# Seven products in place of eight for part of the w_up and gate multiplications of a two-layer encoder trunk

## The chip, the cores and the metric

The kernel runs on one NeuronCore of a Trainium2 chip. The metric is the device time of one execution in microseconds (us); lower is better. TensorE (PE in the profile) multiplies, VectorE (DVE) and ScalarE (ACT) work element by element, GpSimd (POOL) is all but unused here, and the queue of SyncE (SP) issues the loads of the weights.

## What is computed

Two layers of an encoder over 256 tokens of width 2048, all in float32. Cut to what matters here:

```python
proj = x @ w_in                       # 2048 x 10240; its last 4096 columns are gate_A and gate_B
...                                   # two attentions A and B on the other columns
mix = (sigmoid(gate_A) * (A @ w_pa) + sigmoid(gate_B) * (B @ w_pb)) @ w_out
x = layer_norm(alpha * x + mix)
gate, up = split(x @ w_up)            # 2048 x 11264: 5632 columns each
x = layer_norm(alpha * x + (silu(gate) * up) @ w_down)
```

## The kernel before

**Float32 from three products.** Each float32 operand is split into a high part, which TensorE's fast float32 format (fp32r) holds, and a low part, the difference. A product is high x high, high x low and low x high: three matmuls, with x (transposed, 128 features by 128 tokens) as the stationary operand and 512 columns of a weight as the moving one (`rows_product`, lines 215 to 217).

**Pieces.** All the weights are cut into 960 pieces of 512 KB (128 x 1024 a piece), one list in program order. `run` walks it: for piece m it first emits the split of the piece AHEAD_SPLIT places on (`split_to`: ScalarE copies the high part, line 128, VectorE subtracts for the low part, line 129), then the matmuls of piece m, then `post`, what reads a finished accumulator, and then one step of `background`, a list of small tasks (attention, transposes of finished blocks by `turn_block`, the affine step of a LayerNorm). Loads run up to AHEAD_LOAD pieces further on, in a ring of N_RAW buffers. Each engine takes its instructions strictly in this emitted order.

**Buffers.** Split parts, x, transposed blocks and more share N_UNITS units of 4 KB a partition; a writer waits for the last reader of what lay in its unit. PSUM has eight banks: two accumulators of two banks each (one bank for each half of the tokens), which alternate from one multiplication to the next, and four single banks (`aux`) for transposes and attention.

**The places that change.** In `w_up`, chunk c of 512 columns takes the gate block (8 pieces, then silu) and the up block (8 pieces, then the product, line 752); the result is transposed (`turn_block`, line 402; copy and low part at lines 290 and 291, called hT) as the input of `w_down`. `w_down` runs in two parts, after chunks 5 and 10; `residual_gemm` adds to the residual `res`. Where a LayerNorm follows, the last 256 columns are done first for tokens 0 to 127 and then for tokens 128 to 255 (`gemm_a_halves`), so that the first half's LayerNorm lies beside the second half's matmuls. The gates take two such multiplications of 8 pieces for each of four chunks, followed by `merge`: 2 pieces of w_pa and 4 of w_pb. An affine step of two VectorE instructions for each of eight pieces of `res` (lines 436 and 437) is left over for the background in the chunks of `w_up`.

Of the kernel before, what the change touches and what calls it, by code (L numbers as in the profile page):

```python
# [43 lines left out]
EARLY = 3  # L44


def bias_tables():
# [29 lines left out]
def trunk(ctx: ExitStack, tc: tile.TileContext, x, rel_bias, w_in, sink, w_pa, w_pb, w_out,  # L77
# [26 lines left out]

    pieces = []
    background = []
    state = {"load": 0, "split": 0}
    norms = []

    def piece(src, kk, cc, mm, pre=None, post=None):  # L110
        pieces.append(dict(src=src, kk=kk, cc=cc, mm=mm, pre=pre, post=post))
        return pieces[-1]

    def load_to(m):
        while state["load"] < min(m, len(pieces)):
            pc = pieces[state["load"]]
            pc["raw"] = work.tile([P, pc["kk"], pc["cc"]], F32, name="raw", tag="raw", bufs=N_RAW)
            nc.sync.dma_start(pc["raw"], pc["src"])
            state["load"] += 1

    def split_to(m):
        while state["split"] < min(m, len(pieces)):
            load_to(state["split"] + 1 + AHEAD_LOAD)
            pc = pieces[state["split"]]
            raw = pc["raw"]
            hi = unit([P, pc["kk"], pc["cc"]], F32R, "whi")
            lo = unit([P, pc["kk"], pc["cc"]], F32R, "wlo")
            nc.scalar.activation(hi, raw, AF.Copy)  # L128
            nc.vector.tensor_tensor(out=lo, in0=raw, in1=hi.bitcast(F32), op=ALU.subtract)  # L129
            pc["hi"], pc["lo"] = hi, lo  # L130
            state["split"] += 1

    def flush():
        while background:
            background.pop(0)()

    def run():

        for m, pc in enumerate(pieces):
            ahead = min(AHEAD_SPLIT, 1 + m)  # L140
            for n in norms:
                if n - 24 <= m < n:
                    ahead = max(ahead, min(n - m + AHEAD_NORM, AHEAD_SPLIT + (m - n + 24) // 3))
            split_to(m + 1 + ahead)
# [105 lines left out]
    def gemm_a_halves(w, k0, k1, c0, width, xs, post, between):  # L250

        kk = 1024 // width
        st = {"w": []}

        def part(t, j, pc):
            if j == k0:
                st["acc"] = acc_tile()
            for k in range(kk):
                rows_product(st["acc"], t, width, xs(j + k), pc["hi"][:, k, :], pc["lo"][:, k, :],
                             j + k == k0, j + k == k1 - 1)  # L260

        def mm(j, pc):
            part(0, j, pc)
            st["w"].append((j, pc))
            if j + kk >= k1:
                post(0, st["acc"])
                for a in st["w"][:-1]:
                    part(1, *a)
                between()
                part(1, *st["w"][-1])  # L270
                post(1, st["acc"])
        for j in range(k0, k1, kk):
            src = w[j * P:(j + kk) * P, c0:c0 + width].rearrange("(k p) c -> p k c", p=P)
# [133 lines left out]
    def ln_scale(stats, t):  # L407
# [241 lines left out]
    def layer(l, xt, pre, turn, after_last):  # L649
# [67 lines left out]
        def gate(c):  # L717
            for nm, c0 in (("a", GA), ("b", GB)):
                def post(acc, nm=nm):
                    sg[nm] = work.tile([P, 2, 512], F32, name="sg", tag="sg", bufs=3)  # L720
                    nc.scalar.activation(sg[nm], acc, AF.Sigmoid)
                gemm_a(wi, 0, KT, c0 + 512 * c, 512, xs, post)

        def merge(c):
            def post_a(acc):
                nc.vector.tensor_tensor(out=sg["a"], in0=sg["a"], in1=acc, op=ALU.mult)

            def post_b(acc):
                nc.vector.tensor_tensor(out=sg["b"], in0=sg["b"], in1=acc, op=ALU.mult)
                nc.vector.tensor_tensor(out=sg["a"], in0=sg["a"], in1=sg["b"], op=ALU.add)  # L730
                turn_block(sg["a"], mt, "mT")
            gemm_a(w_pa[l], 0, 4, 512 * c, 512, lambda kt: lookup(oa)(kt), post_a, pre=([flush] if c == 0 else None))
            gemm_a(w_pb[l], 0, 8, 512 * c, 512, lambda kt: lookup(ob)(kt), post_b)

        for c in range(4):
            gate(c)
            merge(c)
# [16 lines left out]

        stats2 = small.tile([P, 2, 5, 6], F32, name="stats", tag="stats", bufs=2)
        after2, between2, ret = after_last(stats2)
        for half, (c0, c1) in enumerate(((0, 6), (6, 11))):
            for c in range(c0, c1):
                st = {}
                gemm_a(w_up[l], 0, KT, 512 * c, 512, x1s, lambda acc, st=st: post_gate(acc, st),  # L760
                       turn=(turn1 if c == 0 else None))
                gemm_a(w_up[l], 0, KT, D_FF + 512 * c, 512, x1s, lambda acc, st=st: post_up(acc, st))
            residual_gemm(w_down[l], 4 * c0, 4 * c1, lookup(hs), ALPHA if half == 0 else None,
                          None if half == 0 else stats2, after2, between2)
        if l < DEPTH - 1:
            norms.append(len(pieces))
        return ret
# [80 lines left out]
```

## Time and profile before

| | |
|---|---|
| median of three runs | 2767.43 us (2766.91 to 2768.36) |
| profiled execution | 2767.28 us, span 2765.5 us |
| PE busy | 2749.0 us (99%), 13539 matmuls |
| DVE busy | 1480.9 us (54%) |
| ACT busy | 1168.2 us (42%) |
| granted TensorE clock | 0.998 |

A busy PE is not yet a PE at its peak, since its matmuls overlap: one lasts 390 ns in the profile, while the next starts 227 ns after it. What a matmul costs is therefore read from the starts, not from the durations. Rows with "x6" merge six instructions that follow each other, and the time beside them reaches from the start of the first to the end of the last.

### The profile page before, as it was taken

To read this page: it belongs to the slowest core of one execution; us is meant where nothing else is said; L and a number is where in the kernel's file an instruction comes from. 1 tells how busy PE (TensorE), PEld (TensorE's weight loads), DVE (VectorE), ACT (ScalarE), POOL (GpSimd) and SP (SyncE) were. 2 spreads that over 40 slices of the span, in tenths; PEclk is the share of its full clock that TensorE was granted. 3 is DMA by queue.
4 is the path that set the end of the run, shared out by engine and by line. 5 is a ranking of instruction groups with operands and counts; after the bars stand their busy time and mean duration, and the time that the engine had idled before them with its cause. 6 is when DMAs were issued, how large, how long until landed. Compare 5 with 4: busy or idle time off the path is not lost.

```text
span 2765.5 us, 34763 instructions
## 1 busy us (share of the span) xinstructions
PE 2749.0 (99%) x13539; PEld 2319.5 (84%) x13539; DVE 1480.9 (54%) x1688; ACT 1168.2 (42%) x1407; POOL 5.4 (0%) x13
## 2 busy tenths in 40 slices
PE   9999999999999999999999999999999999999998
PEld 7888888888888888888889888888888888888887
DVE  5566554566644544445566655455665444444445
ACT  4454443444333443434344544433544344423441
POOL 0000000000000000000000000000000000000000
PEclk9999999999999999999999999999999999999999
DMA  8866665564655554655656666555645565555554
GB/s 255 241 183 181 185 202 178 187 229 149 225 184 183 208 204 158 211 177 191 215 162 201 179 183 191 177 201 179 232 162 198 183 205 205 183 183 183 187 209 145
DMA packets 359801, 531.84 MB, mean 192 GB/s; under 512 B 52288, under 2 KB 153664, under 8 KB 359636
## 3 DMA queue, kind: packets, MB, share of 16 engines
q1 hardware_dynamic: 358836, 528.31, 58.1%
q8 instruction: 106, 1.74, 0.3%
q10 hardware_dynamic: 800, 1.31, 0.1%
q14 instruction: 59, 0.48, 0.0%
HBM read 522.86 MB, written 6.68 MB: 191 GB/s over the span
## 4 chain that ended last, share of the span: by engine, by line
PE 98%; DVE 1%; DMA 0%; SPq 0%; issue 0%; ACT 0%; DVEq 0%; POOL 0%; ACTq 0%; POOLq 0%
PE acc L217 27%; PE acc L215 27%; PE acc L216 27%; PE acc L202 9%; PE acc L171 5%; PE aux L402 1%; PE aux L297 0%; PE aux L296 0%; PE aux L295 0%; DVE xT L392 0%; PE aux L562 0%; PE aux L528 0%; PE aux L620 0%; PE aux L544 0%; DMA res<-in_x_dram 0%; PE aux L370 0%
## 5 line engine op out<-in xcount | busy, mean ns | idle before, releaser
L129 DVE TENSOR_TENSOR wlo<-raw,whi 128x1024 fp32r<-128x1024 f32 x960 | 1127.4, 1221 | 474.5 <-ACT whi L128 455.4
L128 ACT ACTIVATE whi<-raw 128x1024 fp32r<-128x1024 f32 x960 | 971.5, 1054 | 434.9 <-DMA raw<-in_w_down_dram 142.1
L215 PE MATMUL acc<-whi,xT 128*128 128x512 f32 (+1 forms) x2176 | 848.7, 390 | 0.0
L217 PE MATMUL acc<-whi,xT 128*128 128x512 f32 (+1 forms) x2176 | 842.0, 387 | 0.0
L216 PE MATMUL acc<-wlo,xT 128*128 128x512 f32 (+1 forms) x2176 | 840.8, 386 | 0.0
L217 PEld LDWEIGHTS acc<-whi,xT 128*128 128x128 f32 x2176 | 409.1, 188 | 84.2
L215 PEld LDWEIGHTS acc<-whi,xT 128*128 128x128 f32 x2176 | 409.3, 188 | 80.8 <-issue 0.7
L216 PEld LDWEIGHTS acc<-wlo,xT 128*128 128x128 f32 x2176 | 409.4, 188 | 80.5
L202 PE MATMUL acc<-xT,whi 128*128 128x512 f32 x1088 | 387.0, 399 | 0.0
L171 PE MATMUL acc<-xT,wlo 128*128 128x256 f32 x1088 | 299.6, 280 | 0.0
L215 PE MATMUL acc<-whi,hT 128*128 128x512 f32 (+1 forms) x784 | 288.9, 368 | 0.0
L217 PE MATMUL acc<-whi,hT 128*128 128x512 f32 (+1 forms) x784 | 288.2, 368 | 0.0
L216 PE MATMUL acc<-wlo,hT 128*128 128x512 f32 (+1 forms) x784 | 288.0, 367 | 0.0
L202 PEld LDWEIGHTS acc<-xT,whi 128*128 128x128 f32 x1088 | 203.0, 188 | 43.3
L171 PEld LDWEIGHTS acc<-xT,wlo 128*128 128x128 f32 x1088 | 205.6, 189 | 2.6
L215 PEld LDWEIGHTS acc<-whi,hT 128*128 128x128 f32 x784 | 147.8, 189 | 24.3
L216 PEld LDWEIGHTS acc<-wlo,hT 128*128 128x128 f32 x784 | 147.9, 189 | 24.3
L217 PEld LDWEIGHTS acc<-whi,hT 128*128 128x128 f32 x784 | 147.8, 189 | 24.3
L290 ACT ACTIVATE hT<-aux 128x512 fp32r<-128x512 f32 x44 | 26.3, 598 | 315.2 <-PE aux L402 315.2
L752 DVE TENSOR_TENSOR sg<-sg,acc 128x1024 f32<-128x1024 f32 x22 | 26.9, 1221 | 202.3 <-PE acc L217 202.3
L215 PE MATMUL acc<-whi,mT 128*128 128x512 f32 (+1 forms) x320 | 111.5, 348 | 0.0
L217 PE MATMUL acc<-whi,mT 128*128 128x512 f32 (+1 forms) x320 | 111.0, 347 | 0.0
(133 smaller groups left out, 1503.8 us busy)
## 6 DMA issues: line engine op xcount, KB each, us to landing
raw<-in_w_up_dram SPq DMA_DIRECT2D x352, 512.0 KB, 4.7
raw<-in_w_in_dram SPq DMA_DIRECT2D x320, 512.0 KB, 4.9
raw<-in_w_down_dram SPq DMA_DIRECT2D x176, 512.0 KB, 5.5
raw<-in_w_out_dram SPq DMA_DIRECT2D x64, 512.0 KB, 5.6
raw<-in_w_pb_dram SPq DMA_DIRECT2D x32, 512.0 KB, 5.0
raw<-in_w_pa_dram SPq DMA_DIRECT2D x16, 512.0 KB, 5.9
bias<-ftab SPq DMA_DIRECT2D x96, 64.0 KB, 3.7
ftab<-fb SPq DMA_DIRECT2D x7, 640.0 KB
```

Source lines behind the costliest of these rows:

```text
L128: nc.scalar.activation(hi, raw, AF.Copy)
L129: nc.vector.tensor_tensor(out=lo, in0=raw, in1=hi.bitcast(F32), op=ALU.subtract)
L171: nc.tensor.matmul(st["acc"][:, n, 0:SEQ], lhsT=lo[:, k, n * P:(n + 1) * P], rhs=xs(4 * j + k)[:, 0, :], start=False, stop=False)
L202: nc.tensor.matmul(acc, lhsT=hi[:, k, n * P:(n + 1) * P], rhs=xs(kt).rearrange("p h t -> p (h t)"), start=first and not turn, stop=last)
L215: nc.tensor.matmul(o, lhsT=xk[:, 0, ts], rhs=hi, start=first, stop=False)
L216: nc.tensor.matmul(o, lhsT=xk[:, 0, ts], rhs=lo, start=False, stop=False)
L217: nc.tensor.matmul(o, lhsT=xk[:, 1, ts], rhs=hi, start=False, stop=last)
L290: nc.scalar.activation(hi, src, AF.Copy)
L402: nc.tensor.transpose(out=ps[:, k, t * P:(t + 1) * P], in_=src[:, t, c0:c0 + P], identity=ident)
L752: nc.vector.tensor_tensor(out=s, in0=s, in1=acc, op=ALU.mult)
```

## The change

The gate block and the up block of one chunk (and gate_A and gate_B of one) are computed together by a new function, `gemm_s`. It takes the 16 row tiles of the weight in eight pairs. With two row tiles, two halves of the tokens and two column blocks, a pair is a product of two 2 x 2 matrices of blocks: eight block products, 24 matmuls. Three of the eight pairs ("S" in PLAN) are done by Strassen's method (Winograd's form) with seven products, 21 matmuls; the five others ("C") as before. An S pair is four entries in the list of pieces, two with a load and two without. VectorE makes the sums of the weight's blocks (t13, t24) and their low parts; the sums of x (`sum_rows`) are made once for each x. The seven products go to all eight banks: q1, q5, q6, q7 to the four aux banks, q2 and q3 to one accumulator, q4 and x (the fourth plain result) to the other. After the last S pair, `fold` turns q1, q5, q6 and q7 into four corrections (e, f), and after the last pair each of the four banks is added to its correction (line 414). In the S pairs and the C pairs between them no background step runs ("quiet").

26 of the 30 pairs of blocks are done in this way: chunks 1 to 10 of `w_up` and chunks 1 to 3 of the gates, in both layers. Besides, the splits run five pieces ahead in place of three, with seven raw buffers and 36 units; transposes of finished blocks go into a list of their own that is served first (`soon`); and `w_down` runs in three parts (4, 4 and 3 chunks) in place of two, so the last part, with its 256-column ends, has 12 row tiles in place of 20.

```diff
-N_RAW = 6
-N_UNITS = 37
+N_RAW = 7
+N_UNITS = 36
+SUMS = 3
+PLAN = "SCSCSCCC"
-AHEAD_SPLIT = 3
+AHEAD_SPLIT = 5
...
-            if background:
-                background.pop(0)()
+            if not pc.get("quiet") and (soon or background):
+                (soon or background).pop(0)()
...
+        names = {"S": ("q1", "q2", "q3", "q5", "q7", "q6", "q4"),
+                 "C": ("q2", "q2", "q4", "q4", "q3", "q3", "x", "x")}
...
+            def split1(pc):
+                split_plain(pc)
+                b["left"] = pc["raw"]
+            def split2(pc):
+                raw = b["right"] = pc["raw"]
+                b["t13"] = unit([P, 2, 512], F32, "t13")
+                nc.vector.tensor_tensor(out=b["t13"][:, 0, :], in0=b["left"][:, 0, :], in1=raw[:, 0, :], op=ALU.add)
+                b["b22"] = unit([P, 2, 512], F32R, "b22")
+                split_into(b["b22"][:, 0, :], b["b22"][:, 1, :], raw[:, 1, :])
...
+            def split3(pc):
+                b["t24"] = unit([P, 2, 512], F32, "t24")
+                for o, x0, x1 in ((b["t13"][:, 1, :], b["right"][:, 0, :], b["right"][:, 1, :]),
+                                  (b["t24"][:, 0, :], b["t13"][:, 0, :], b["right"][:, 1, :])):
+                    nc.vector.tensor_tensor(out=o, in0=x0, in1=x1, op=ALU.add)
+                nc.vector.tensor_tensor(out=b["t24"][:, 1, :], in0=b["t24"][:, 0, :], in1=b["left"][:, 1, :], op=ALU.add)
+                b["h13"] = halves(b["t13"])
+            def split4(pc):
+                b["h24"] = halves(b["t24"])
...
+        def fold():
+            e, f, d = unit([P, 2, 512], F32, "e"), unit([P, 2, 512], F32, "f"), work.tile([P, 512], F32, name="tmp", tag="tmp", bufs=2)
+            nc.scalar.activation(e[:, 0, :], st["q1"], AF.Copy)
+            nc.vector.tensor_tensor(out=d, in0=e[:, 0, :], in1=st["q6"], op=ALU.subtract)
+            nc.vector.tensor_tensor(out=e[:, 1, :], in0=d, in1=st["q7"], op=ALU.subtract)
+            nc.vector.scalar_tensor_tensor(f[:, 0, :], st["q5"], -1.0, d, op0=ALU.mult, op1=ALU.subtract)
+            nc.vector.scalar_tensor_tensor(f[:, 1, :], st["q5"], -1.0, e[:, 1, :], op0=ALU.mult, op1=ALU.subtract)
...
+                for t, n in enumerate(names_):
+                    for k in range(2):
+                        product(n, rows(2 * p + k, t), pc["hi"][:, k, :], pc["lo"][:, k, :])
+                    if last:
+                        nc.vector.tensor_tensor(out=out_[:, t, :], in0=st[n], in1=st[extra][:, t, :], op=ALU.add)
...
-        background.extend([lambda: None, lambda: half(0), lambda: half(1)])
+        soon.extend([lambda: None, lambda: half(0), lambda: half(1)])
...
-        for half, (c0, c1) in enumerate(((0, 6), (6, 11))):
+        chunks = ((0, 4), (4, 8), (8, 11))
+        for part, (c0, c1) in enumerate(chunks):
             for c in range(c0, c1):
                 st = {}
...
+                if c > 0:
+                    gemm_s(w_up[l], 512 * c, D_FF + 512 * c, x1s, sums, post_both)
+                    continue
```

**TensorE at the end of a chunk of w_up.** Before, the next block starts in the other accumulator at once (acc_7032 is the finished one).

```order
L215 MATMUL acc_7032<-whi_7101,xT_5502 128x512
L216 MATMUL acc_7032<-wlo_7102,xT_5502 128x512
L217 MATMUL acc_7032<-whi_7101,xT_5502 128x512
L215 MATMUL acc_7178<-whi_7119,xT_5495 128x512
L216 MATMUL acc_7178<-wlo_7120,xT_5495 128x512
L217 MATMUL acc_7178<-whi_7119,xT_5495 128x512
```

Now (acc_8145 and acc_8146 are the banks of this chunk, acc_8501 and acc_8502 the same two pairs of banks for the next one, b22, thi and tlo the high and low parts of the weight's sums, sT a sum of x):

```order
L331 MATMUL acc_8146<-whi_8364,xT_5664 128x512
L329 MATMUL aux_8503<-whi_8390,xT_5657 128x512
L330 MATMUL aux_8503<-wlo_8391,xT_5657 128x512
L331 MATMUL aux_8503<-whi_8390,xT_5657 128x512
L329 MATMUL acc_8501<-whi_8390,xT_5657 128x512
L330 MATMUL acc_8501<-wlo_8391,xT_5657 128x512
L331 MATMUL acc_8501<-whi_8390,xT_5657 128x512
L329 MATMUL acc_8501<-b22_8418,sT_5885 128x512
L329 MATMUL aux_8526<-thi_8439,sT_5885 128x512
L330 MATMUL aux_8526<-tlo_8440,sT_5885 128x512
```

Only the three matmuls into an aux bank (q1) now stand between the end of a chunk and the first matmul into the pair of banks whose adds have just been emitted.

**VectorE around the end of a chunk of w_up.** Before, the product (line 752), two transposed blocks and low parts alone:

```order
L752 TENSOR_TENSOR sg<-sg,acc 128x1024
L129 TENSOR_TENSOR wlo<-raw,whi 128x1024
L291 TENSOR_TENSOR hT<-aux,hT 128x2x256
L129 TENSOR_TENSOR wlo<-raw,whi 128x1024
L291 TENSOR_TENSOR hT<-aux,hT 128x2x256
L129 TENSOR_TENSOR wlo<-raw,whi 128x1024 x14
```

Now, from behind the four instructions of `fold` up to the first two final adds (t_8416 is t13, t_8435 is t24 and b_8418 is b22 of the next chunk's first S pair):

```order
L470 TENSOR_TENSOR wlo<-raw,whi 128x1024
L470 TENSOR_TENSOR hT<-aux,hT 128x2x256
L470 TENSOR_TENSOR wlo<-raw,whi 128x1024
L470 TENSOR_TENSOR hT<-aux,hT 128x2x256
L354 TENSOR_TENSOR t_8416<-raw 128x512
L470 TENSOR_TENSOR b_8418<-raw,b_8418 128x512
L367 TENSOR_TENSOR t_8416<-raw 128x512
L367 TENSOR_TENSOR t_8435<-t_8416,raw 128x512
L368 TENSOR_TENSOR t_8435<-t_8435,raw 128x512
L470 TENSOR_TENSOR tlo<-t_8416,thi 128x1024
L470 TENSOR_TENSOR tlo<-t_8435,thi 128x1024
L414 TENSOR_TENSOR sg<-acc,e 128x512 x2
```

The sums and splits of the next chunk's first S pair stand in front of the final adds of this chunk.

## Rows read from the trace of the kernel before

**Rows 1.** The page, busy time: engine, us (share), instructions.

```profile
PE 2749.0 (99%) x13539; PEld 2319.5 (84%) x13539; DVE 1480.9 (54%) x1688; ACT 1168.2 (42%) x1407; POOL 5.4 (0%) x13
```

**Rows 2.** The page, chain that ended last: shares of the span by engine.

```profile
PE 98%; DVE 1%; DMA 0%; SPq 0%; issue 0%; ACT 0%; DVEq 0%; POOL 0%; ACTq 0%; POOLq 0%
```

**Rows 3.** Chain in order of time, twice 36 rows: start, us, what.

```profile
765.99 0.23 PE acc L215
...
773.92 0.23 PE acc L217
...
775.96 0.23 PE acc L217
...
783.89 0.23 PE acc L216
```

**Rows 4.** Stretches: start:end, length, busy PE, PEld, DVE, ACT, POOL, clock, DMA share, GB/s.

```profile
743.94:788.43 44.49, 44.49 (x202) 36.81 (x201) 21.13 (x19) 17.73 (x19) 0.00 (x0) 1.00 0.55 189
766.00:774.00 8.00, 8.00 (x37) 6.60 (x37) 8.00 (x7) 6.20 (x7) 0.00 (x0) 1.00 0.70 235
776.00:784.00 8.00, 8.00 (x37) 6.61 (x36) 0.00 (x0) 0.00 (x0) 0.00 (x0) 1.00 0.53 197
```

**Rows 5.** Chain again, the transposes that bound that chunk.

```profile
743.94 0.44 PE aux L402 x4
...
788.43 0.44 PE aux L402 x4
```

**Rows 6.** Timeline of DVE, same chunk: start, us, engine, what, [idle before, releaser].

```profile
749.20 6.90 DVE L129 TENSOR_TENSOR wlo<-raw,whi 128x1024 fp32r<-128x1024 f32 x6 [0.26 <-ACT whi L128]
765.99 8.04 DVE L129 TENSOR_TENSOR wlo<-raw,whi 128x1024 fp32r<-128x1024 f32 x7 [9.89 <-ACT whi L128]
```

**Rows 7.** Timeline of DVE, an affine step of the LayerNorm among splits.

```profile
701.49 0.68 DVE L436 TENSOR_TENSOR res<-res,gb 128x512 f32<-128x512 f32 x1
702.21 0.69 DVE L437 TENSOR_TENSOR res<-res,gb 128x512 f32<-128x512 f32 x1
702.82 2.35 DVE L129 TENSOR_TENSOR wlo<-raw,whi 128x1024 fp32r<-128x1024 f32 x2
```

**Rows 8.** Timeline of ACT, the chunk of rows 4.

```profile
747.62 0.60 ACT L290 ACTIVATE hT<-aux 128x512 fp32r<-128x512 f32 x1 [1.60 <-PE aux L402]
748.11 5.79 ACT L128 ACTIVATE whi<-raw 128x1024 fp32r<-128x1024 f32 x6
```

**Rows 9.** Groups by form: what, xcount, busy us, mean ns, idle before, releaser.

```profile
L128 ACT ACTIVATE whi<-raw 128x1024 fp32r<-128x1024 f32 x960 | 971.5, 1054 | 434.9 <-DMA raw<-in_w_down_dram 142.1 <-DMA raw<-in_w_up_dram 94.2 <-PE acc L217 66.3
L446 DVE SCALAR_TENSOR_TENSOR res<-res,acc 128x512 f32<-128x512 f32 x2 | 1.4, 689 | 6.6 <-PE acc L217 6.6
```

**Rows 10.** Timeline of DVE and ACT, first half's LayerNorm at the end of layer 0.

```profile
1376.42 0.42 DVE L444 TENSOR_TENSOR res<-res,acc 128x256 f32<-128x256 f32 x1 [3.46 <-PE acc L217]
1378.55 1.00 DVE L426 TENSOR_SCALAR res<-res,mv,rstd 128x512 f32<-128x512 f32 x2
1378.67 1.52 ACT L422 ACTIVATE res<-res,shift,rstd 128x512 f32<-128x512 f32 x2 [11.57 <-DVE shift L417]
```

**Rows 11.** Chain there, and near the end of the program.

```profile
1382.14 0.45 PE aux L377 x4
...
2751.95 0.12 PE acc L215
...
2754.71 0.13 PE acc L217
...
2754.86 0.43 DVE res L444
```

**Rows 12.** Timeline of DVE near the end of the program.

```profile
2747.67 0.42 DVE L444 TENSOR_TENSOR res<-res,acc 128x256 f32<-128x256 f32 x1 [3.47 <-PE acc L217]
...
2752.96 1.41 DVE L786 SCALAR_TENSOR_TENSOR res<-res,rstd,gb 128x512 f32<-128x512 f32 x2
```

**Rows 13.** Timeline of ACT at the start of the program.

```profile
24.65 1.06 ACT L128 ACTIVATE whi<-raw 128x1024 fp32r<-128x1024 f32 x1 [1.24 <-DMA raw<-in_w_in_dram]
```

More of the change, by code (lines that the diff above doesn't have):

```diff
@@ L106, in trunk @@
     background = []
-    state = {"load": 0, "split": 0}
+    soon = []
+    state = {"load": 0, "split": 0, "add": 0, "add_load": 0}
     norms = []
     def piece(src, kk, cc, mm, pre=None, post=None):
-        pieces.append(dict(src=src, kk=kk, cc=cc, mm=mm, pre=pre, post=post))
+        pieces.append(dict(src=src, kk=kk, cc=cc, mm=mm, pre=pre, post=post, split=split_plain))
         return pieces[-1]
@@ L116, in load_to, with split_plain, raw_tile, add_to @@
             pc = pieces[state["load"]]
-            pc["raw"] = work.tile([P, pc["kk"], pc["cc"]], F32, name="raw", tag="raw", bufs=N_RAW)
-            nc.sync.dma_start(pc["raw"], pc["src"])
+            if pc["src"] is not None and not pc.get("added"):
+                raw_tile(pc)
             state["load"] += 1
+    def split_plain(pc):
+        raw = pc["raw"]
+        pc["hi"] = unit(list(raw.shape), F32R, "whi")
+        pc["lo"] = unit(list(raw.shape), F32R, "wlo")
+        split_into(pc["hi"], pc["lo"], raw)
+    def raw_tile(pc):
+        pc["raw"] = work.tile([P, pc["kk"], pc["cc"]], F32, name="raw", tag="raw", bufs=N_RAW)
+        nc.sync.dma_start(pc["raw"], pc["src"])
+    def add_to(m):
+        while state["add_load"] < min(m + AHEAD_ADD_LOAD, len(pieces)):
+            pc = pieces[state["add_load"]]
+            if pc and pc.get("added"):
+                raw_tile(pc)
+            state["add_load"] += 1
+        while state["add"] < min(m + AHEAD_ADD, len(pieces)):
+            pc = pieces[state["add"]]
+            if pc and pc.get("added"):
+                raw = pc["raw"]
+                pc["hi"], pc["lo"] = unit(list(raw.shape), F32R, "whi"), unit(list(raw.shape), F32R, "wlo")
+                nc.scalar.activation(pc["lo"], raw, AF.Copy, scale=-1.0)
+                nc.gpsimd.dma_start(pc["lo"], raw, accum_op=ALU.add)
+                nc.scalar.activation(pc["hi"], raw, AF.Copy)
+                pc["split"] = lambda pc: None
+            state["add"] += 1
     def split_to(m):
@@ L124, in split_to @@
             pc = pieces[state["split"]]
[L125 to L130, printed above, removed]
+            pc["split"](pc)
             state["split"] += 1
@@ L733, in merge, with both, post @@
             gemm_a(w_pb[l], 0, 8, 512 * c, 512, lambda kt: lookup(ob)(kt), post_b)
-        for c in range(4):
-            gate(c)
-            merge(c)
+        xsums = []
+        def both(c):
+            def post(a, b):
+                for nm, v in (("a", a), ("b", b)):
+                    nc.scalar.activation(v, v, AF.Sigmoid)
+                    sg[nm] = v
+            gemm_s(wi, GA + 512 * c, GB + 512 * c, xs, xsums, post)
+        for c in range(4):
+            if c == 0:
+                gate(c)
+                merge(c)
+                pieces[-6]["pre"] = lambda: (flush(), soon.extend([
+                    lambda i=i: xsums.append(sum_rows(xt[i])) for i in range(SUMS)]))
+            else:
+                both(c)
+                merge(c)
         stats1 = small.tile([P, 2, 5, 6], F32, name="stats", tag="stats", bufs=2)
@@ L756, in layer, with post_both @@
         after2, between2, ret = after_last(stats2)
[L757 removed]
+        sums = []
+        def post_both(gate_, up_):
+            nc.scalar.activation(gate_, gate_, AF.Silu)
+            nc.vector.tensor_tensor(out=gate_, in0=gate_, in1=up_, op=ALU.mult)
+            turn_block(gate_, hs, "hT")
+        chunks = ((0, 4), (4, 8), (8, 11))
+        for part, (c0, c1) in enumerate(chunks):
             for c in range(c0, c1):
                 st = {}
[L760 to L761 removed]
+                if c > 0:
+                    gemm_s(w_up[l], 512 * c, D_FF + 512 * c, x1s, sums, post_both)
+                    continue
+                gemm_a(w_up[l], 0, KT, 512 * c, 512, x1s, lambda acc, st=st: post_gate(acc, st), turn=turn1)
                 gemm_a(w_up[l], 0, KT, D_FF + 512 * c, 512, x1s, lambda acc, st=st: post_up(acc, st))
[L763 to L764 removed]
+                pieces[-12]["pre"] = lambda: background.__setitem__(slice(0, 0), [
+                    lambda i=i: sums.append(sum_rows(x1t[i])) for i in range(SUMS)])
+            last = part == len(chunks) - 1
+            residual_gemm(w_down[l], 4 * c0, 4 * c1, lookup(hs), ALPHA if part == 0 else None,
+                          stats2 if last else None, after2, between2)
         if l < DEPTH - 1:
```

91 lines of the change are left out of this document (added).

## The prediction

> **What bounds the kernel now.** First the busy times: PE is busy 99% of the span, DVE 54%, ACT 42% [rows 1]. Then the chain that ended last: 98% of it is PE [rows 2]. So time is saved by taking matmuls off PE, and lost wherever PE is made to wait. What a matmul costs is read from starts, not from durations: 36 matmuls that follow each other start 7.93 us apart from the first to the last, so one takes 7.93 / 35 = 0.2266 us, whether DVE works all through the stretch or not at all [rows 3, 4]. A chunk of w_up (192 matmuls of 512 columns, 8 transposes at 0.11) is then 43.5 + 0.9 = 44.4 us; the trace shows 44.49 between two such transposes [rows 5]. In it DVE is busy 21.13 us and ACT 17.73 [rows 4]. PE waits for neither of them there, so the question is what remains of DVE's spare 23 us.
>
> **The matmuls removed.** An S pair has 21 matmuls for 24. 26 chunks x 3 pairs x 3 = 234 matmuls x 0.2266 = **-53.0 us**. All are on the path, since PE is.
> The Trainium skill (TensorE: Matmul & The Clock Gate, Wait - 56ns, not 53.3ns?) gives 215.7 ns from start to start for 512 columns; by that the term would be -50.5 and the time 2.5 us longer, but the trace shows 226.6 and I take that.
>
> The third part of w_down shortens the 256-column ends: in both layers together 192 matmuls of 0.12 us (24 rows in 2.76 us, [rows 11]) become 96 of 0.2266: -23.0 + 21.8 = **-1.3 us**. The four residual updates that a third part adds in each layer are DVE work of 1.2 us each, beside a stage where DVE is half idle: nothing.
>
> **What DVE must do in such a chunk.** Prices: 1024 columns, back to back, (6.90 - 1.22) / 5 = 1.137 us [rows 6]; 512 columns 702.82 - 702.21 = 0.61, or 0.72 where the next instruction needs the result (702.21 - 701.49) [rows 7]; operands in PSUM cost the same (689 ns for 512, [rows 9]). An S pair on DVE: low part of the left block 1.14, first sum and low part of b22 1.22, then three sums 0.61 + 0.61 + 0.72, low part of t13 1.2 (it stands behind two sums, which hide ACT's 1.05 us copy of t13, [rows 9]), low part of t24 1.14: together 6.6 us, against 21 x 0.2266 = 4.76 on PE. A C pair is 2.27 on DVE, 5.44 on PE. The chunk: DVE 3 x 6.6 + 5 x 2.27 + fold 2.7 + four final adds 2.6 + product 1.1 + two hT 1.2 = 38.9 us; PE 3 x 4.76 + 5 x 5.44 + 0.9 = 42.4. So DVE goes from 47% to 92% of such a chunk and is not yet the bound on average. ACT, with 0.95 us a copy back to back [rows 8], comes to some 24 us: nothing.
>
> An average doesn't settle it, because DVE is strictly in order and three times in a chunk it waits for PE. I walk one chunk from the start of its first S pair (0), pieces 0 to 21 in the order S C S C S C C C.
> (a) Up to the fold. DVE ends the last add of the chunk before (0.8), the product (2.0), and splits pieces 5 to 20: two S pairs, eight C pieces: 2.0 + 13.2 + 9.1 = 24.3. PE ends its third S pair at 3 x 4.76 + 2 x 5.44 = 25.2. DVE is there 0.9 us early.
> (b) From the fold to the first final adds, the place of the order rows. Fold to 27.9, a low part 29.0, hT 29.6; the next low part waits for ACT, which copies the hT block first (transposed at 28.3, copied 0.6 [rows 8]), and ends at 31.2; the second hT block is transposed by 31.5, and its low part ends at 32.8; the rest of the S pair 5.5: 38.3. PE ends the q2 products at 25.2 + 0.9 + 4 x 2.72 + 1.36 = 38.3. The first add runs 38.4 to 39.1, and PE needs its bank pair at 39.7, after q4's six matmuls: 0.6 us to spare.
> (c) The handover. q4's add, one low part (1.1) and q3's add end at 42.2. The next S chunk needs that pair of banks after q1's three matmuls, at 43.0; w_pa or w_down needs it at 42.4, at once. It just holds.
> So a plain handover costs **0**, with 0.2 to 0.9 us of cover at each place; if the cover is gone, PE waits by what DVE is late.
>
> **Handovers with an affine step.** In chunks 1 to 3 of w_up a pair of instructions of 0.72 + 0.61 = 1.33 us [rows 7] stands ahead of the first adds, and another between q4's add and the low part. After chunks 1 and 2 PE then waits 1.33 - 0.6 = 0.8 at (b) and some 0.4 at (c); after chunk 3, where the splits are light ones of w_down, only 1.1 at (c). Two layers: 2 x (1.2 + 1.2 + 1.1) = **+7 us**; ends 0 (DVE a little faster than its rows) and 13 (twice as late). I take 7, as it comes from the walk.
>
> **The end of the program.** The first half's LayerNorm occupies DVE from 2747.67 to 2752.96 + 1.41 = 2754.37, 6.7 us [rows 12]. It lay beside the second half's 60 matmuls, 7.2 us, and PE's last matmul ended with DVE free [rows 11]. Now there are 36, 4.3 us, and the second half's LayerNorm starts 6.7 - 4.3 = **+2.4 us** late. What it then waits for is DVE alone.
> At the end of layer 0 the same cover sinks from 5.7 (1376.4 to 1382.14) to 2.9 us before the first transposes [rows 10, 11]. The residual blocks are ready 3.0 to 3.1 us after 1376.4 (DVE's two until 1379.55, the first of ACT's two at 1379.4, [rows 10]): **+0.2 us**; then the chain is the old one.
>
> **Splits five ahead.** At the start, two splits more stand in front of the last blocks of x, and ACT there waits for loads (1.24 us, [rows 13]): **+0.5**, ends 0 and 1.5. Elsewhere 36 units hold: a split's unit was last read by matmuls six to eight pieces earlier. Loads: 8.4 MB a chunk in 42.4 us are 198 GB/s, and 235 were moved in a stretch [rows 4]; the raw ring runs some 10 us ahead of the splits: nothing. The list `soon` and the quiet pieces only delay hT to the sixth last piece of the next chunk, long before w_down reads it: nothing.
>
> **The sum.** -53.0 - 1.3 + 7 + 2.4 + 0.2 + 0.5 = -44.2. From the profiled execution's own 2767.28 us (its span is 2765.5, and the median of the runs 2767.43, so it is a typical one): **2723 us**. Without the waits of the affine steps and the start it is 2715.6; with the upper ends 2730.
>
> **Rivals.**
> 1. *DVE is late at the handover.* If back-to-back DVE instructions don't overlap as in rows 6 where sums, hT and PSUM operands mix, each of the 45 costs its whole duration and a gap, 0.12 us more (1.22 + 0.04 for 1.137). The chunk is then 38.9 + 5.4 = 44.3 on DVE against 42.4 on PE, and PE waits 1.9 us at the first final add wherever an S chunk follows an S chunk, 14 times (chunks 1-2, 2-3, 4 to 7 and 8 to 10, two layers). +26: 2749 us. It decides from 0.08 us an instruction. For it: the sums are dependent. Against it: rows 6 and 7 show the overlap with waits on ACT and loads in every instruction.
> The Trainium skill (VectorE: DVE Perf Modes, The DRAIN you can't avoid) says that the next instruction doesn't start until the pipe is empty; by that rule this rival would hold, but 1.137 from start to start for a duration of 1.22 speaks against it here.
> 2. *DVE becomes the bound and the change loses.* The same place, with DVE at 0.2 us an instruction over its rows, because ACT's copies, the loads and DVE's two operands meet in the same buffers: 47.9 us a chunk, 14 x 5.5 = +77: 2800 us. It passes the old time from 45.5 us a chunk, 0.15 an instruction. Rows 6 were taken with ACT copying and 235 GB/s of loads at the same time [rows 4, 8], without a sign of this.
> 3. *PE gains nothing.* The matmuls in S pairs alternate between banks and stationaries; 1638 of them would need 0.254 us in place of 0.2266 to eat the 44 us: 2767 us. Rows 3 alternate stationaries too, at a steady step.
>
> **Chances.** The forecast, with its ends 2714 to 2732: 0.70. Rival 1, whole or in part, 2732 to 2750: 0.20. Rival 2: 0.05. Rival 3, or several small losses that cancel the gain: 0.03. Faster than 2714: 0.02. The range is 2714 to 2746, which leaves out rivals 2 and 3, the tail of rival 1 and the fast end. A measurement of this kernel can tell about 0.2% (5.5 us) from no change: faster 0.92, the same 0.03, slower 0.05.
>
> **What the profile after would show.** PE: 330 matmuls fewer in all, the step in an S chunk 0.2266, and a chunk of w_up from transpose to transpose about 42.4 us. DVE: some 1980 us busy and about 39 of 42.4 in such a chunk. The chain still over 96% PE. Waits of PE for line 414 only after chunks 1 to 3 of w_up, around 1 us each; waits after the other chunks speak for rival 1, and a DVE step over 1.2 us for low parts back to back for rival 2. The last PE instruction should stand some 2.4 us further from the end than before. The forecast is wrong if PE waits for low parts in the middle of a chunk, which the walk excludes by several us.

## The result, and the profile after

| | before | after |
|---|---|---|
| median of the runs | 2767.17 us (2766.57 to 2768.36) | 2732.03 us (2731.35 to 2732.77) |
| profiled execution | 2767.28 us, span 2765.5 | 2732.01 us, span 2730.2 |
| ratio of the times | | 0.9873, 95% interval 0.9855 to 0.989 |

The change gains 35 us; 44 had been forecast. So the question is not only why it is faster but where 9 us of the gain stayed.

The busy times of the page after, against [rows 1]: 330 matmuls fewer, as predicted, and DVE up to 1979.5 us (1980 predicted).

```profile
PE 2699.5 (99%) x13209; PEld 2268.1 (83%) x13209; DVE 1979.5 (73%) x2432; ACT 1305.1 (48%) x1601; POOL 5.4 (0%) x13
```

The gain is read between the first transposes of two neighbouring chunks of w_up, as in [rows 4, 5]. Two such chunks after, with busy time (and instructions) of PE, PE's weight loads, DVE, ACT and POOL, then the granted clock, the share of the DMA engines and GB/s:

```profile
983.90:1026.36 42.46, 42.46 (x193) 35.13 (x192) 39.09 (x46) 23.00 (x26) 0.00 (x0) 1.00 0.62 200
1026.36:1068.81 42.45, 42.45 (x192) 35.13 (x191) 39.09 (x46) 23.00 (x26) 0.00 (x0) 1.00 0.61 197
```

42.45 us for the 44.49 of before, PE without a gap, DVE busy 39.09 of it (forecast: 42.4 and 38.9). If all 26 chunks gain what these two do, that is 26 x 2.04 = 53.0 us: the whole term of the removed matmuls.

What stayed behind is in the waits. What PE waited for in the whole program after, the seven largest of ten rows (total us, times, longest):

```profile
PE acc L329 <- DVE sg L908: 2.9, 2, 1.4
PE acc L329 <- DVE sg L414: 2.5, 4, 0.6
PE aux L549 <- DMA res<-in_x_dram: 2.5, 2, 1.8
PE acc L245 <- DVE sg L414: 2.4, 2, 1.2
PE aux L330 <- DVE tlo L470: 1.6, 2, 0.8
PE aux L527 <- DMA hots<-const_hot_dram: 1.5, 1, 1.5
PE aux L556 <- DVE res L605: 1.5, 3, 0.5
```

The transposes' waits for res (L549, L556) were there before. L414 is the final additions, the handovers that the prediction spoke of. After chunk 1 of w_up they look so on DVE (start, duration, instruction; in brackets idle time before it and what ended that):

```profile
732.69 0.68 DVE L615 TENSOR_TENSOR res<-res,gb 128x512 f32<-128x512 f32 x1
733.40 0.69 DVE L616 TENSOR_TENSOR res<-res,gb 128x512 f32<-128x512 f32 x1
734.02 1.22 DVE L470 TENSOR_TENSOR tlo<-t,thi 128x1024 fp32r<-128x1024 f32 x1
735.15 1.28 DVE L414 TENSOR_TENSOR sg<-acc,e 128x512 f32<-128x512 f32 x2
```

The affine pair (L615, L616) holds the additions up by 1.33 us, 732.69 to 734.02, and PE's wait there is 0.635. L908 and tlo are not in the prediction; both stand in one place, the first S chunk of the gates in each layer:

```profile
381.50 0.50 PE L330 MATMUL aux<-tlo,sT 128*128 128x512 f32 x1 [0.79 <-DVE tlo L470]
...
385.06 0.51 PE L329 MATMUL acc<-thi,xT 128*128 128x512 f32 x1 [1.43 <-DVE sg L908]
```

Measured from start to start, these two steps are 1.06 and 1.60 us longer than a matmul. Here is why, first ACT and then DVE ahead of them:

```profile
361.95 1.03 ACT L900 ACTIVATE sg<-acc 128x1024 f32<-128x1024 f32 x1 [8.50 <-PE acc L247]
```

DVE in the same stretch:

```profile
349.70 5.77 DVE L470 TENSOR_TENSOR wlo<-raw,whi 128x1024 fp32r<-128x1024 f32 x5 [0.52 <-ACT whi L469]
363.96 1.23 DVE L470 TENSOR_TENSOR wlo<-raw,whi 128x1024 fp32r<-128x1024 f32 x1 [8.49 <-ACT whi L469]
365.10 0.68 DVE L444 TENSOR_TENSOR v<-xT 128x512 f32<-128x512 f32 x1
...
380.23 2.51 DVE L470 TENSOR_TENSOR tlo<-t,thi 128x1024 fp32r<-128x1024 f32 x2
...
383.79 1.22 DVE L908 TENSOR_TENSOR sg<-sg,acc 128x1024 f32<-128x1024 f32 x1
```

ACT stands 8.5 us at the sigmoid of gate 0, which waits for PE's last product; the copies of the next piece stand behind it in order, and DVE idles 8.49 us for those. Only then do the three sums of x, the first S pair and the two products of merge fall on DVE together, between 365 and 385, and it comes late for tlo and for the bank pair that L908 still reads. The place looks harmless in a busy share and is decided by the order on two engines.

### The profile page after: what moved, and what is told of

Read it like the earlier page. It is cut to its first block, busy times and chain, and to the rows that moved or that the text cites. A ratio compares the mean times of both kernels' runs of the same rounds, so it can differ in the third digit from the quotient of the medians.

```text
span 2730.2 us, 35012 instructions
## 1 busy us (share of the span) xinstructions
PE 2699.5 (99%) x13209; PEld 2268.1 (83%) x13209; DVE 1979.5 (73%) x2432; ACT 1305.1 (48%) x1601; POOL 5.4 (0%) x13
## 5 line engine op out<-in xcount | busy, mean ns | idle before, releaser
L470 DVE TENSOR_TENSOR wlo<-raw,whi 128x1024 fp32r<-128x1024 f32 x882 | 1039.3, 1220 | 153.7 <-ACT whi L469 110.9
L469 ACT ACTIVATE whi<-raw 128x1024 fp32r<-128x1024 f32 x882 | 889.2, 1051 | 271.3 <-PE acc L247 132.4
L329 PE MATMUL acc<-whi,xT 128*128 128x512 f32 x1118 | 440.3, 394 | 2.5 <-DVE sg L414 2.5
L331 PE MATMUL acc<-whi,xT 128*128 128x512 f32 x1118 | 435.9, 390 | 0.0
L330 PE MATMUL acc<-wlo,xT 128*128 128x512 f32 x1118 | 435.1, 389 | 0.0
L469 ACT ACTIVATE thi<-t 128x1024 fp32r<-128x1024 f32 x156 | 165.8, 1063 | 373.2 <-DVE t L367 352.0
L329 PEld LDWEIGHTS acc<-whi,xT 128*128 128x128 f32 x1118 | 210.0, 188 | 47.3 <-issue 4.1
L331 PEld LDWEIGHTS acc<-whi,xT 128*128 128x128 f32 x1118 | 209.8, 188 | 44.6
L330 PEld LDWEIGHTS acc<-wlo,xT 128*128 128x128 f32 x1118 | 210.0, 188 | 42.3
L245 PE MATMUL acc<-whi,xT 128*128 128x512 f32 (+1 forms) x512 | 195.9, 383 | 1.0 <-ACT xT L469 1.0
L247 PE MATMUL acc<-whi,xT 128*128 128x512 f32 (+1 forms) x512 | 193.1, 377 | 0.6 <-DVE xT L470 0.6
L470 DVE TENSOR_TENSOR tlo<-t,thi 128x1024 fp32r<-128x1024 f32 x156 | 190.5, 1222 | 4.1 <-ACT thi L469 0.3
L246 PE MATMUL acc<-wlo,xT 128*128 128x512 f32 (+1 forms) x512 | 192.6, 376 | 0.0
```

The costliest lines, as they stand in the source:

```text
L245: nc.tensor.matmul(o, lhsT=xk[:, 0, ts], rhs=hi, start=first, stop=False)
L246: nc.tensor.matmul(o, lhsT=xk[:, 0, ts], rhs=lo, start=False, stop=False)
L247: nc.tensor.matmul(o, lhsT=xk[:, 1, ts], rhs=hi, start=False, stop=last)
L329: nc.tensor.matmul(o, lhsT=xk[0], rhs=hi, start=first, stop=False)
L330: nc.tensor.matmul(o, lhsT=xk[0], rhs=lo, start=False, stop=False)
L331: nc.tensor.matmul(o, lhsT=xk[1], rhs=hi, start=False, stop=last)
```

## The experiments

All are edits of the changed kernel. Times are medians, against the kernel before, measured beside it (2767.3 to 2768.0).

**1. The rest of the change without Strassen's method.** The S chunks computed as before, and no sums of x:

```
-                both(c)
+                gate(c)
                 merge(c)
...
-                if c > 0:
-                    gemm_s(w_up[l], 512 * c, D_FF + 512 * c, x1s, sums, post_both)
-                    continue
```

> Strassen's method taken out again; the rest of the change stays (five ahead, `soon`, w_down in three parts). Theory M (PE sets the time; the 9 us missing are waits of PE in and beside the S chunks, where DVE is nearly full): 2767.2 - 1.3 (256-column ends) + 2.3 (end of the program) + 1.8 (start) = 2770, between 2768 and 2772, and no wait of PE for DVE at the handovers of w_up, since DVE is half idle again. Rival G (the 9 us are lost by the new order itself, in splits five ahead, transposes and the third part, all through the program): 2767.2 - 1.3 + 9 = 2775 or more. Rival P (an S pair saves less than three matmul steps, and something else gains): 2763 to 2766.

2771.28 us, ratio 1.0012 (1.0003 to 1.0021). No wait for DVE at a handover; the last matmul ends 12.9 us from the end (10.7 before). Theory M holds: the moves around the method cost 4 us and do not hold the missing 9. The method alone is worth 2732.0 - 2771.3 = -39.3.

**2. Two S pairs in a chunk** (`PLAN = "SCSCCCCC"`, `SUMS = 2`).

> S in two of eight pairs, plan SCSCCCCC, sums of two tiles of x. Theory M: 26 x 3 x 0.2266 = 17.7 us more of matmuls than after; DVE has 4.3 us less in a chunk that is 0.7 us longer, so the waits at the handovers with affine steps (6.0) should go and those in the first S chunk of the gates (5.3) shrink to 2 to 3: 2732 + 17.7 - 6 - 2.5 = 2741, between 2738 and 2745. Rival G (what is missing is spread evenly, not DVE's): 2732 + 17.7 - 3 (a third of the 9) = 2747, between 2746 and 2750. Rival P (the third S pair of a chunk was worth less than its three matmuls, since it fills DVE): below 2738.

2738.62 us, ratio 0.9895 (0.9881 to 0.9908). At the fast edge of M, outside G, and 0.6 us from P. PE waits for the final additions only twice:

```profile
PE acc L329 <- DVE sg L414: 0.9, 2, 0.4
```

and in the first S chunk of the gates not at all. So of the 17.7 us of matmuls that the third S pair removes only 6.6 arrive: 5.3 go in the gates' first S chunk and 4.7 at the handovers with affine steps (6.0 against 1.2), which leaves 7.7, a microsecond from what was measured. So P's thought, that a third pair brings less than its matmuls because it fills DVE, is right at these places.

**3. Four S pairs** (`PLAN = "SCSSCSCC"`, `SUMS = 4`).

> S in four of eight pairs, plan SCSSCSCC, sums of four tiles of x. Theory M: DVE has 43.2 to 43.4 us of work in a chunk, PE 41.8; DVE is the bound where an S chunk follows an S chunk (14 places), and with 3.4 us of waits for ACT that it has in a chunk today the chunk is 43 to 46 us: 2732 - 12 x 0.7 + 14 x (0.7 to 3.5) = 2733 to 2773, most likely 2745, with waits of PE for DVE in every S chunk. Rival PE (DVE at 92% has room still, waits come from extra work only): 2732 - 17.7 = 2714.

2766.30 us, ratio 0.9995 (0.9986 to 1.0003): the whole gain is gone. M's direction is right, its likeliest value (2745) too low. The waits of PE for the final additions:

```profile
PE acc L329 <- DVE sg L414: 31.6, 26, 2.1
```

The busy times of a chunk of w_up from one such wait's end to the next, and of 4 us behind the second (columns as above):

```profile
1005.23:1049.16 43.93, 42.06 (x189) 34.49 (x189) 42.86 (x52) 24.49 (x28) 0.00 (x0) 1.00 0.59 192
1049.50:1053.50 4.00, 4.00 (x12) 3.13 (x11) 2.02 (x3) 3.48 (x4) 0.00 (x0) 0.58 0.36 91
```

DVE is the bound: busy 42.86 us of 43.93, while PE waits in every one of the 26 chunks. Against after, the steps of PE give: matmuls -17.7, waits at L414 +31.5, for thi and tlo +6.3, the start and single steps +3, and 56 matmuls at 0.42 us in place of 0.227, +11.0: together +34. That last item no theory had; it is taken up at the end.

**4. Splits three ahead** (`AHEAD_SPLIT = 3`).

> Splits three ahead again, all else as after. Theory M: DVE comes to the fold two C pieces (4.5 us of work) earlier, idles there, and has them to do later; 39.1 + 4.5 = 43.6 against 42.45, so PE waits about 1 to 3 us in each of the 14 S chunks that follow another, and the start is 1 to 1.8 us shorter: 2732 - 1.5 + 14 to 42 = 2745 to 2772. Rival D (the depth hides nothing that PE needs): 2730 to 2731, the shorter start alone.

2766.86 us, ratio 0.9996 (0.9987 to 1.0005): the depth is worth 35 us, as much as the whole change. The time is inside M, and the waits for L414 are at the 14 places that M named. PE's largest waits:

```profile
PE acc L329 <- DVE sg L414: 20.0, 14, 2.4
PE aux L330 <- DVE tlo L470: 4.0, 4, 1.6
```

Behind some of these waits 28 matmuls, in four stretches, start 0.42 us apart in place of 0.227, as in experiment 3: some 5.5 us that M did not have.

**5. Affine steps into w_down.** After the first block's two steps, nine pops of the background list do nothing, so the other three blocks' steps fall into w_down's first part:

```
             for c in range(4):
                 background.append(lambda c=c: load(c))
+                if c == 1:
+                    background.extend([lambda: None] * 9)
```

> The affine steps of the last three blocks of x leave w_up's chunks 1 to 3 for the first part of w_down, where DVE is busy 20 us of 42. Theory M: the four waits of 0.80 us (place b) and the two of 1.38 us (after chunk 3) go, all of them DVE's affine work: 2732 - 6 = 2726, between 2725 and 2727.5. Rival H (the cover at the handover is nil anyhow, the affine steps only show it): the waits shrink to 0.3 to 0.5 us or turn up one place later, 2728.5 to 2732.

2725.32 us, ratio 0.9849 (0.9834 to 0.9863): -6.7. No wait of PE for L414 is left anywhere in the trace; rival H falls.

**6. Sums for the gates earlier.**

```
-                pieces[-6]["pre"] = lambda: (flush(), soon.extend([
-                    lambda i=i: xsums.append(sum_rows(xt[i])) for i in range(SUMS)]))
+                pieces[-11]["pre"] = lambda: soon.extend([
+                    lambda i=i: xsums.append(sum_rows(xt[i])) for i in range(SUMS)])
```

> The three sums of x for the gates are made eleven pieces ahead of the first S chunk's end of cover (three pieces before gate 0 ends, where DVE stands idle 8.5 us behind ACT's sigmoid) in place of in w_pa. Theory M: both waits of that S chunk (1.06 for a low part, 1.60 for the banks that L908 still reads) are DVE's queue, 2 x 2.66 = 5.3 us: 2732 - 5.3 = 2726.7, between 2725.5 and 2728. Rival (the first is ACT's copy of the sums, the second the accumulator's order; DVE's queue is not it): 2731 to 2732, with waits of the same size.

2726.71 us, ratio 0.9854 (0.9839 to 0.9869): -5.3. Both waits are gone. On DVE the sums now stand in the idle time, and L908 is the one that waits, for PE:

```profile
350.75 0.68 DVE L444 TENSOR_TENSOR v<-xT 128x512 f32<-128x512 f32 x1
...
378.18 1.22 DVE L908 TENSOR_TENSOR sg<-sg,acc 128x1024 f32<-128x1024 f32 x1 [1.83 <-PE acc L247]
```

**7. Three splits ahead at the start, five later.**

```
-            ahead = min(AHEAD_SPLIT, 1 + m)
+            ahead = min(AHEAD_SPLIT if m >= 24 else 3, 1 + m)
```

> Three splits ahead in the first 24 pieces, five after that. Theory M: the waits for xT (1.27 and 0.81) and for hots (1.66) in the first 48 us are from the two splits and loads more that stand in front: 2732 - 1.8 to - 3.7 = 2728.3 to 2730.2. Rival (the start is as it was, and differs from run to run): 2731 to 2733.

2730.42 us, ratio 0.9866 (0.9852 to 0.9881): -1.6, less than M said, from medians of four executions that lie up to 2.1 us apart. The wait for hots (1.66) is gone, as in the other three runs with three splits ahead (4, 9 and 11); with five it shows in all runs but experiment 1. The waits for xT stayed (0.94 and 0.81), so the depth alone does not make them.

But the profiled execution itself gained little at the start. The 1200th matmul of the trace, the same instruction in every run, starts at 217.85 us before, at 219.62 after and at 219.37 here, where PE waits 1.0 us for low parts in the first 48 us, which it does not do after. In the eight other runs that keep the start of after it starts at 218.5 to 221.7, and with three splits ahead at 215.9 to 220.3. So what the rival says of the start, that it differs from run to run, is true as well: executions differ there by more than the term, and its size is not settled.

**8. The last part of w_down with 16 row tiles** (`chunks = ((0, 3), (3, 7), (7, 11))`).

> w_down in parts of 12, 16 and 16 row tiles in place of 16, 16 and 12. Theory M: the second half's 48 matmuls of 256 columns cover 5.8 us of the first half's 6.7 us of LayerNorm: tail -1.4; 32 matmuls of 256 columns more, 16 of 512 fewer: +0.2; one handover with affine steps less in each layer, -1.6: 2732 - 2.8 = 2729, between 2728 and 2730.5, and the last PE instruction 11.5 us from the end in place of 13.0. Rival (the end waits for ACT or the output's transfers, the cover is no matter): 2730.5 to 2732.5, and the last PE instruction 13.0 us from the end.

2729.69 us, ratio 0.9865 (0.9848 to 0.9881): -2.3, at M's slow end. The last PE instruction, in a span of 2727.7:

```profile
2715.97 0.28 PE L247 MATMUL acc<-whi,hT 128*128 128x256 f32 x1
```

and that of after, in one of 2730.2:

```profile
2716.95 0.28 PE L247 MATMUL acc<-whi,hT 128*128 128x256 f32 x1
```

11.5 us and 13.0 us from the end, as M said: what covers the first half's LayerNorm are the second half's matmuls.

**9. Edits 5 to 8 together** (in 5, six empty pops for nine, since the first part of w_down now follows chunk 2).

> The four edits of the runs before together: affine steps in w_down, sums for the gates earlier, three splits ahead at the start, w_down in parts of 12, 16 and 16. If each takes away a wait of its own (theory M): 2732 - 6.7 - 5.3 - 1.6, and of the 2.3 of the shorter part only the tail's 1.2, since its handover is gone already: 2717, between 2715.5 and 2719, no wait of PE for DVE from the first gate to the end but those before the LayerNorm's transposes. If the waits give way to others one place later: 2720 to 2725.

2716.90 us, ratio 0.9816 (0.9801 to 0.9831), 15 us faster than after. All that PE still waits for:

```profile
PE aux L549 <- DMA res<-in_x_dram: 1.6, 2, 0.9
PE acc L245 <- ACT xT L469: 1.5, 1, 1.5
PE aux L556 <- DVE res L605: 1.5, 3, 0.5
PE acc L496 <- DVE zeros L1015: 1.1, 1, 1.1
PE acc L247 <- DVE xT L470: 0.6, 1, 0.6
```

The gains add up to what was expected (2717), and none of the waits came back one place later. DVE still works 73% of the span: some 12 of the 15 us (experiments 5 and 6) were lost by its order, not by its load; the others lay at the start and at the end.

**10. A dose of DVE work behind the fold.** In each S chunk:

```
             st["e"], st["f"] = e, f
+            for _ in range(2):
+                nc.vector.tensor_tensor(out=d, in0=e[:, 0, :], in1=e[:, 1, :], op=ALU.add)
```

> After as it is, with two DVE additions of 512 columns (0.61 us each, unused results) behind the fold of each S chunk, 1.2 us of DVE work and nothing else. Theory M, with a cover of 0.7 us before the first final adds (1.33 us of affine steps gave a wait of 0.635): 0.5 + 0.17 at 10 plain S to S handovers, 1.2 at the 4 with affine steps, 1.2 after chunk 3 and 0 to 1.1 before the other w_down and w_pa stages: 2732 + 6.7 + 4.8 + 2.4 + 0 to 11 = 2746 to 2757, most likely 2750. Rival N (no cover at all, every DVE instruction in an S chunk is on the path): 26 x 1.2 = 31 and the restarts, 2763 or more. Rival W (DVE has the whole 3.4 us of idle time to give): 2732 to 2737.

2731.51 us, ratio 0.9869 (0.9854 to 0.9884): it costs nothing; from the 1200th matmul to the end the trace is within 0.1 us of after's. M's lower end is missed by 14.5 us, its likeliest value by 18.5, and W, which was next to no cost, comes closest. DVE from the fold on in after:

```profile
1025.75 1.22 DVE L470 TENSOR_TENSOR wlo<-raw,whi 128x1024 fp32r<-128x1024 f32 x1
1027.62 0.69 DVE L470 TENSOR_TENSOR hT<-aux,hT 128x512 fp32r<-128x512 f32 x1 [0.65 <-ACT hT L469]
1028.57 1.23 DVE L470 TENSOR_TENSOR wlo<-raw,whi 128x1024 fp32r<-128x1024 f32 x1 [0.26 <-ACT whi L469]
1030.83 0.69 DVE L470 TENSOR_TENSOR hT<-aux,hT 128x512 fp32r<-128x512 f32 x1 [1.03 <-ACT hT L469]
```

and with the dose (its line numbers are two higher):

```profile
1024.89 1.41 DVE L406 TENSOR_TENSOR tmp<-e 128x512 f32<-128x512 f32 x2
1026.22 1.22 DVE L472 TENSOR_TENSOR wlo<-raw,whi 128x1024 fp32r<-128x1024 f32 x1
1027.35 0.69 DVE L472 TENSOR_TENSOR hT<-aux,hT 128x512 fp32r<-128x512 f32 x1
1027.95 1.22 DVE L472 TENSOR_TENSOR wlo<-raw,whi 128x1024 fp32r<-128x1024 f32 x1
1029.77 0.69 DVE L472 TENSOR_TENSOR hT<-aux,hT 128x512 fp32r<-128x512 f32 x1 [0.60 <-ACT hT L471]
```

The 1.33 us of the dose went into the idle time before the two hT blocks (0.65 + 0.26 + 1.03 = 1.94 in after, 0.60 with the dose). PE's transposes set when DVE goes on from there, not what DVE did before.

**11. Four S pairs with help from GpSimd**, on top of experiment 9: two of the four sums of weights of an S pair on the idle engine.

```
-                nc.vector.tensor_tensor(out=b["t13"][:, 0, :], ...
+                nc.gpsimd.tensor_tensor(out=b["t13"][:, 0, :], ...
```

(likewise `b["t13"][:, 1, :]`; SUMS = 4 and PLAN = "SCSSCSCC"; and one empty pop fewer ahead of the first affine step.)

> All the edits of e9_all, S in four of eight pairs, and two of the four sums of weights of an S pair on GpSimd. DVE has 42.9 us of work in such a chunk without that; with 8 sums of 0.61 off it, 38. If GpSimd's sums are ready in time and slow DVE in nothing: PE sets the chunk at 41.8, 2717 - 17.7 = 2700, between 2698 and 2705. If DVE's instructions become slower beside GpSimd's (or wait for them), DVE or GpSimd sets the chunk: from 42.5 us on nothing is gained, at 43.9 it is 2740 or more.

2800.67 us, ratio 1.0121 (1.0104 to 1.0138), the second case. POOL (GpSimd) in a stretch of w_up:

```profile
1005.96 1.43 POOL L354 TENSOR_TENSOR t<-raw 128x512 f32<-128x512 f32 x1 [5.75 <-PE acc L331]
1007.36 1.74 POOL L365 TENSOR_TENSOR t<-raw 128x512 f32<-128x512 f32 x1
```

DVE in the same stretch:

```profile
1006.16 1.78 DVE L366 TENSOR_TENSOR t<-t,raw 128x512 f32<-128x512 f32 x1
1007.98 1.67 DVE L367 TENSOR_TENSOR t<-t,raw 128x512 f32<-128x512 f32 x1
...
1015.98 0.69 DVE L366 TENSOR_TENSOR t<-t,raw 128x512 f32<-128x512 f32 x1
```

The same DVE instruction (L366) takes 0.69 us alone and 1.78 beside a sum on POOL; on average L366 takes 0.976 us over 104. A sum on POOL costs 1.63 to 1.95 us (means of 104), and what it takes off DVE it takes back: 208 sums of some 0.6 us have left DVE, and yet it is busy 2135 us, against 2093 in experiment 3. PE now waits for the final additions for 54.3 us, up to 4.4 at a time. The Trainium skill (SBUF — State Buffer, SBUF: two separate sides) says that a GpSimd instruction that reads SBUF and a DVE instruction with two SBUF inputs exclude each other for a whole instruction; the trace agrees: the two DVE instructions of 1.78 and 1.67 us end 0.55 us behind the end of the POOL sum that they lie beside.

**12. The same dose in front of the first final addition**, behind both hT blocks:

```
                 if last:
                     out_ = work.tile([P, 2, 512], F32, name="sg", tag="sg", bufs=3)
+                if last and extra == "e":
+                    tmp = work.tile([P, 512], F32, name="tmp", tag="tmp", bufs=2)
+                    for _ in range(2):
+                        nc.vector.tensor_tensor(out=tmp, in0=st["e"][:, 0, :], in1=st["e"][:, 1, :], op=ALU.add)
```

> After as it is, with the same two DVE additions (1.2 us) not behind the fold but in front of the first final add of each S chunk, behind both hT blocks. The dose behind the fold went into DVE's waits for ACT's copies of hT (0.65, 0.26 and 1.03 us in the chunk of 983.90 to 1026.36); from the second hT block on, DVE has no such wait before the first final add. Theory M': there the cover is 1.33 - 0.635 = 0.70 us, as the affine steps show: 0.5 + 0.17 at the 10 plain S to S handovers, 1.2 at the 4 with affine steps, 0 to 1.2 after chunk 3 and nothing at the other w_down and w_pa stages, where light splits stand in front of the adds: 2731.8 + 6.7 + 4.8 + 0 to 2.4 = 2743 to 2746. Rival C (DVE has more cover there too, and the waits with affine steps come from the step between the adds): 2732 to 2737. Rival N (every DVE instruction behind the hT blocks is on the path): 26 x 1.2 + restarts, 2763 or more.

2744.82 us, ratio 0.9917 (0.9904 to 0.9931), inside M'. The waits (L418 is L414 of after):

```profile
PE acc L329 <- DVE sg L418: 13.7, 14, 2.0
```

Six are at plain handovers, 0.72 us each; the dose takes 1.33 us there, so the cover is 0.61 us, and the prediction's walk had 0.6 at (b). Six and not ten, since the handovers from chunk 4 to 5 and 8 to 9, just behind w_down, show none; instead one turns up in each layer's gates (0.45) and one at chunk 3's first final additions (0.31 and 0.39). The four with affine steps went from 0.63 to 1.96, by the whole dose, while the later wait after chunk 3 fell from 1.2 to 0.7. So M' has the total right, and the place and size of the cover, but not every place of the waits.

## Why the prediction was right, and where it was not

The time lay in the predicted range, 9 us above the forecast. It is 2 us beyond the sum's own upper end (2730), and at 2732 it stands on the border between the band given to the forecast and the one given to the first rival. So the number alone does not tell which of them was right; the waits do. Term by term:

| term | forecast | measured |
|---|---|---|
| 234 matmuls removed | -53.0 | -53.0 (26 x 2.04 from transpose to transpose) |
| 256-column ends | -1.3 | not apart; within the +4.0 of experiment 1 |
| plain handovers | 0 | 0 (no such wait; cover 0.61, experiment 12) |
| handovers with affine steps | +7 | +6.0 by the starts of PE, 6.7 by experiment 5 |
| end of the program | +2.4 | +2.3 (10.7 to 13.0 us; 1.5 back in experiment 8) |
| end of layer 0 | +0.2 | no wait beyond those of before |
| start | +0.5 | +1.8 between these two executions (1200th matmul); not settled (experiment 7) |
| first S chunk of the gates | none | +5.3 (experiment 6: all of it) |

The measured terms, with -1.3 taken as it was, make -38.9 of the -35.3 between the profiled executions. 3.6 us stay unassigned; 2.4 of them are 28 more single steps of PE that are 0.06 to 0.15 us over the usual. Counted from the 1200th matmul to the end, which leaves the start out, the trace of experiment 5 is 7.5 us shorter than after's and that of experiment 6 is 6.2: 1.5 and 0.9 more than the waits in the table. So some 2 of the 3.6 us seem to belong to the handovers with affine steps and to the gates' first S chunk as well.

**The mechanism was right, and so were most of the sizes.** A matmul of the S pairs takes what others take (0.2272 from start to start, 0.2271 before), so the rival that PE gains nothing falls. DVE's back-to-back prices hold: five low parts end after 5.77 us, (5.77 - 1.22) / 4 = 1.14 each, as in [rows 6]. They hold with sums and PSUM operands mixed in, too. Two neighbours of the fold in after, which read PSUM (aux), and two in an S pair, the second of them a sum:

```profile
1024.55 0.68 DVE L402 SCALAR_TENSOR_TENSOR f<-aux,tmp 128x512 f32<-128x512 f32 x1
1025.15 0.68 DVE L403 SCALAR_TENSOR_TENSOR f<-aux,e 128x512 f32<-128x512 f32 x1
...
1032.04 0.68 DVE L470 TENSOR_TENSOR b<-raw,b 128x512 fp32r<-128x512 f32 x1
1032.64 0.68 DVE L367 TENSOR_TENSOR t<-raw 128x512 f32<-128x512 f32 x1
```

The two of a pair start 0.60 us apart and last 0.68. So the rival of a late DVE at plain handovers doesn't act. The Trainium skill (VectorE: DVE Perf Modes, The DRAIN you can't avoid) has the next instruction start only when the pipe is empty, but adds that one that is not held starts earlier; the prediction used the first half alone. The step of 1.14 for a duration of 1.22 agrees with the second half for these. The second rival, DVE as the bound, is true one step further: with four S pairs the prediction's own prices give 38.9 + 6.6 - 2.27 = 43.2 us of DVE, and the chunk takes 43.9. DVE is then the bound by its amount of work, not by slower instructions, as that rival had it. Among two, three and four S pairs a chunk, three is the best.

**The walk at the handover** was right in place and size at (b): 0.6 us forecast, 0.61 measured. At (c) it had 0.4 us after chunks 1 and 2, and there was none; after chunk 3 it had 1.1, and it was 1.38. What the walk didn't say is that the cover is a thing of a place: 1.33 us of DVE work cost nothing behind the fold, and 0.9 at six of the ten plain handovers where it stood some 11 us later.

**The step that failed** is a place left out. The part on splits five ahead and the list `soon` priced everything outside the S to S handovers at nothing ("Elsewhere 36 units hold", "the list `soon` ... nothing"), and no term stood for entering the S chunks for the first time, where the sums of x, an S pair and merge's products meet on DVE behind an ACT that is held by a sigmoid. That is 5.3 of the 9 us. The start was put at 0.5 with an end of 1.5, and took 1.8 between the two profiled executions. Part of it has the term's cause (two splits more in front), though the wait that goes with three splits ahead is for another load (hots); how much of it the depth costs stays open, since executions with the same start differ by 3 us there.

**The signs that were named.** 330 matmuls, 42.4 us, some 1980 us of DVE and 2.4 us at the end all showed. Waits for L414 stood after chunks 1 to 3 alone, at 0.80, 0.80 and 1.38 us. The share of PE in the chain could not be read: the chain of after that the page follows back ends in DVE's last 15 us.

## What to carry to other kernels

Where work is moved onto an engine up to nine tenths of its time, price not only the steady repetition but each entry into it and each thing that is already queued there: here the repetition cost nothing, and one entry in each layer and six handovers took 11 us, all of which came back by moving DVE work of the same amount to where it stood idle. An idle share of an engine in order can be used only where it lies; a dose of extra work, put at two places, measures it directly. And a good time with one such plan says nothing of its neighbours: one S pair more, or two splits ahead less, cost the entire gain.

## What the runs showed of the hardware

**PE's clock fell after waits of under 2 us in a stretch in which PE was otherwise busy.** Matmuls in experiment 3 around the second of the waits above:

```profile
1049.16 0.56 PE L329 MATMUL acc<-whi,xT 128*128 128x512 f32 x1 [1.86 <-DVE sg L414]
1049.52 0.63 PE L330 MATMUL acc<-wlo,xT 128*128 128x512 f32 x1
1049.95 0.63 PE L331 MATMUL acc<-whi,xT 128*128 128x512 f32 x1
...
1053.14 0.39 PE L330 MATMUL acc<-wlo,xT 128*128 128x512 f32 x1
```

The starts are 0.43 us apart at first, the step of 1.2 GHz, and 0.23 after 1053, that of 2.4; the granted clock of that stretch is 0.58. So the eight matmuls behind a wait of 1.86 us took some 1.6 us more. It happens after some waits only: the one at 1005.23, as long, was followed by none of it, nor were the waits of 1.96 in experiment 12. In experiment 3 it took 11.0 us in all (56 matmuls), in experiment 11 19.0 (98), in experiment 4 some 5.5 (28), and after, where the longest wait between the start and the end is 1.43 us, nothing. What decides it was not tried.

**GpSimd and DVE did not work side by side** on additions of this kind: a DVE addition of 0.69 us took 1.78 beside one on GpSimd (experiment 11).
